# Router logits by token half in a two-layer decoder trunk, and the order of the steps up to the first gather

## The chip, the cores and the metric

The kernel runs on one core of a Trainium2 chip, alone. The metric is the device time of one execution in microseconds; the median of several runs counts. One further execution was recorded by the hardware profiler, and all rows below are from it. TensorE does the matrix products, VectorE and ScalarE the elementwise work, POOL (GpSimd) a little of it, and SyncE (SP) issues nearly all transfers.

## The reference, cut to what matters

The trunk has two layers with 256 tokens of width 1024, all in float32. A layer is a mixer of three branches, a cross-attention into 256 memory tokens, and a feed-forward part, each followed by a layer norm of `alpha * x + f(x)`. In the first layer the feed-forward part is dense; in the second one, which the change is about, it is a mixture of 8 experts with the best 2 taken for each token:

```python
def moe_swiglu(x, w_router, b_router, w_gu, w_down):
    logits = (x @ w_router).astype(jnp.float32) + b_router.astype(jnp.float32)
    top_vals, top_idx = lax.top_k(logits, TOP_K)
    top_w = jax.nn.softmax(top_vals, axis=-1)
    combine = jnp.sum(jax.nn.one_hot(top_idx, N_EXPERTS, dtype=jnp.float32) * top_w[..., None], axis=-2)
    out = jnp.zeros_like(x)
    for e in range(N_EXPERTS):
        out = out + combine[..., e:e + 1].astype(x.dtype) * swiglu(x, w_gu[e], w_down[e])
    return out
```

Here `x` is the output of the norm behind the cross-attention, `y * g + b` with `y` the normalized rows and `g`, `b` one value per channel.

## The kernel before, in words

**Precision by two parts.** A float32 operand of a big product is split into `hi`, its value rounded to the fast matmul type, and `lo`, the residual `raw - hi`; a product is three matmuls, hi x hi, hi x lo and lo x hi. The weights come as 1 MB tiles (`raw`, L242 to L256) by SyncE's queue. Each is used in halves of 128x1024: ScalarE makes `whi` (L218), VectorE makes `wlo` (L221). There are three buffers of each. In the last layer the raw tiles go through a long ring of 15 buffers, so that transfers run far ahead.

**The order.** A planner places the instructions of each engine by priority (mostly program order) and by its own estimate of durations, so an instruction of later code fills a gap where its inputs are there. Code under `tc.high_priority()` goes first; both norms and all that they call are written so. A `Line` (L230 to L239) pins a chain by hand: each call is issued behind the one before it on its engine. The norm has four such chains, `dv` for VectorE, `ac` for ScalarE, `te` for TensorE and `gp` for POOL. Instructions called through a Line are recorded at L238. `guard` (L225, L270) holds the next weight residuals back behind a given instruction of VectorE: the norm sets it to the next two, behind `shift(1)` (L343).

**The norm ahead of the experts** (`layer_norm_in`, L310, with kind "moe", called from `cross` at L1109). Tokens are in two halves, m = 0 and 1, with 128 tokens on the partitions. For each half VectorE adds up `y = alpha * x + f` (tile `lny`) and takes its statistics, POOL raises the variance to the power -0.5 (`brs`), and VectorE makes the shift (`bnb`, L327). ScalarE normalizes the rows in place (L347); TensorE transposes them by 128x128 blocks into four PSUM tiles, which hold two channel blocks of both halves each (L351). The affine part is then applied to the transposed blocks, one 128x256 operation per channel block, five on ScalarE and three on VectorE (`lnx`, L364 to L367), and TensorE takes the logits transposed, 8 experts on the partitions by 256 tokens: eight products with an 8-column stationary and 256 columns streamed (`pl`, L369). The affine part of the rows themselves (`x`, needed for the gather and the residual path) is done by POOL for half 0 (L354, L355) and by VectorE for half 1 (L356, L380). ScalarE rounds them to `xhi` (L382).

**The router** (`moe`, L1170). VectorE copies the logits from PSUM (`lgt`), TensorE transposes them back (L1189), VectorE adds the bias row (`lg`), compares all pairs (`eq`, `cmp`), sums to `rank` and takes `sel`, the two best. TensorE counts earlier tokens of each expert by triangular and all-ones matrices (L1213 to L1215); VectorE makes the token's `slot` in its expert, and `pe`, the 128x128 selection matrices (L1258, recorded at L238). The residuals of the rows, `xlo`, are made one in the shade of the counting (L1216) and one behind `pe` (L1260). `prepare` (L1253) gathers the rows of two experts by matmuls with `pe` (L1273), 16 with `xhi` and 16 with `xlo`; ScalarE and VectorE carry the results into `xg` (the casts). `weigh` (L1227) computes the two weights, and POOL scales `x` by alpha for the last norm (L1250).

**The experts.** For each of 8 experts and 7 blocks of 512 hidden columns, `gate_up` (L1292) runs two chains `pg` and `pu` over four weight halves each, then SiLU and product (`msl`); `down` (L1317) projects back, and `scatter` (L1329) adds the weighted rows to `x`.

**The earlier norm of the same layer.** Behind the mixer the norm of kind "xt" runs, with cross-attention keys as filling; then `cross` (L1043) does the last block of keys (L1052) and the query projection (L1054).

## Time and profile before

| | |
|---|---|
| median of 3 runs | 1942.06 us (1941.7 to 1943.23) |
| the profiled execution's own time | 1947.3 us |
| its span, first to last instruction | 1945.4 us |
| TensorE busy in the span | 1882.1 us (97%) |
| VectorE busy | 1532.6 us (79%) |
| ScalarE busy | 1283.2 us (66%) |
| POOL busy | 110.9 us (6%) |
| mean granted TensorE clock | 0.984 |

The engines' names in the rows are PE for TensorE's matmuls, PEld for its weight loads, DVE for VectorE, ACT for ScalarE, POOL for GpSimd and SP for SyncE. A matmul row gives rows * columns of the stationary operand and then partitions x columns of the result. A busy TensorE in these rows is not TensorE at its peak: matmuls overlap, and their ends are modelled. Times in the timelines are from the span's start; a merged row "x3" runs from the first start to the last end.

### The profile page before, as it was taken

Reading aid. Unit: us, or ns where it says so; the run is one execution under the profiler, and the core shown is the slowest. Engines: PE = TensorE matmul, PEld = TensorE weight load, DVE = VectorE, ACT = ScalarE, POOL = GpSimd, SP = SyncE. Lnnn points to the kernel's source line nnn. Section 1 sums busy time; section 2 is a strip of 40 time slices with the busy share of each in tenths; the row PEclk is TensorE's granted clock in tenths of the full one; section 3 lists DMA queues with packets and bytes.
Section 4 is the critical chain, followed back from the end, with each engine's and each line's share of the span. In section 5 each row is a group of like instructions: output and inputs, shape, how many; then the busy total and the mean of one; then the engine's idle time right before and its main releaser. Section 6 shows DMA issues by size and latency. Waiting matters only on the chain.

```text
span 1945.4 us, 27894 instructions
## 1 busy us (share of the span) xinstructions
PE 1882.1 (97%) x10672; PEld 1634.6 (84%) x10672; DVE 1532.6 (79%) x1976; ACT 1283.2 (66%) x1673; POOL 110.9 (6%) x111
## 2 busy tenths in 40 slices
PE   7999999999999999989899999999999999999996
PEld 7998998899989988877688888888888888888875
DVE  7774764794557755755899999999999999999987
ACT  5666554555444555544678787887777778788774
POOL 4030000100004300000200000000000000000000
PEclk9999999999999999989899999999999999999998
DMA  7324553544554343594499998999989999899970
GB/s 255 131 93 153 185 216 134 182 171 163 185 188 170 130 145 121 194 378 173 174 371 371 359 373 320 375 373 355 375 318 375 375 354 374 318 375 368 382 274 24
DMA packets 74924, 503.37 MB, mean 259 GB/s; under 512 B 9504, under 2 KB 11808, under 8 KB 15264
## 3 DMA queue, kind: packets, MB, share of 16 engines
q1 hardware_dynamic: 74496, 500.43, 68.6%
q8 instruction: 85, 1.39, 0.3%
q0 software_dynamic: 144, 1.05, 0.2%
q14 instruction: 55, 0.45, 0.1%
q10 hardware_dynamic: 144, 0.05, 0.0%
HBM read 498.34 MB, written 1.05 MB: 257 GB/s over the span
## 4 chain that ended last, share of the span: by engine, by line
PE 87%; DVE 8%; ACT 3%; issue 2%; DMA 0%; POOL 0%; ACTq 0%; DVEq 0%; POOLq 0%
PE ps L281 8%; PE ps L283 8%; PE ps L282 8%; PE pu L1302 5%; PE dn L450 5%; PE pu L1303 5%; PE pu L1301 5%; PE pg L1303 5%; PE pg L1302 5%; PE dn L451 5%; PE dn L452 5%; PE pg L1301 5%; DVE wlo L221 3%; PE acc L428 2%; PE acc L430 2%; PE acc L432 2%
## 5 line engine op out<-in xcount | busy, mean ns | idle before, releaser
L221 DVE TENSOR_TENSOR wlo<-raw,whi 128x1024 fp32r<-128x1024 f32 x926 | 1118.3, 1229 | 308.4 <-ACT whi L218 295.3
L218 ACT ACTIVATE whi<-raw 128x1024 fp32r<-128x1024 f32 x926 | 974.4, 1060 | 519.3 <-PE ps L282 187.5
L281 PE MATMUL ps<-xhi,whi 128*128 128x256 f32 x992 | 288.3, 291 | 14.8 <-ACT whi L218 14.8
L283 PE MATMUL ps<-xhi,wlo 128*128 128x256 f32 x992 | 286.4, 290 | 4.3 <-DVE wlo L221 4.3
L282 PE MATMUL ps<-xlo,whi 128*128 128x256 f32 x992 | 286.8, 289 | 0.0
L281 PEld LDWEIGHTS ps<-xhi,whi 128*128 128x128 f32 x992 | 194.8, 197 | 16.3 <-ACT whi L218 15.5
L283 PEld LDWEIGHTS ps<-xhi,wlo 128*128 128x128 f32 x992 | 194.8, 197 | 5.8 <-DVE wlo L221 5.1
L282 PEld LDWEIGHTS ps<-xlo,whi 128*128 128x128 f32 x992 | 195.3, 197 | 0.8 <-issue 0.3
L1302 PE MATMUL pu<-wlo,xg 128*128 128x512 f32 x448 | 176.1, 393 | 2.7 <-DVE wlo L221 2.7
L451 PE MATMUL dn<-wlo,hth 128*128 128x512 f32 x448 | 178.0, 400 | 0.1
L1302 PE MATMUL pg<-wlo,xg 128*128 128x512 f32 x448 | 176.6, 394 | 1.4 <-DVE wlo L221 1.4
L1303 PE MATMUL pg<-whi,xg 128*128 128x512 f32 x448 | 175.8, 392 | 0.6 <-DVE xg L1254 0.6
L1301 PE MATMUL pg<-whi,xg 128*128 128x512 f32 x448 | 175.2, 391 | 0.0
L1301 PE MATMUL pu<-whi,xg 128*128 128x512 f32 x448 | 175.1, 391 | 0.0
L1303 PE MATMUL pu<-whi,xg 128*128 128x512 f32 x448 | 174.8, 390 | 0.0
L452 PE MATMUL dn<-whi,htl 128*128 128x512 f32 x448 | 174.0, 391 | 0.0
L450 PE MATMUL dn<-whi,hth 128*128 128x512 f32 x448 | 139.5, 391 | 0.0
L1302 PEld LDWEIGHTS pu<-wlo,xg 128*128 128x128 f32 x448 | 84.1, 188 | 27.6 <-DVE wlo L221 6.6
L1302 PEld LDWEIGHTS pg<-wlo,xg 128*128 128x128 f32 x448 | 84.1, 188 | 24.1 <-DVE wlo L221 3.8
L1301 PEld LDWEIGHTS pu<-whi,xg 128*128 128x128 f32 x448 | 84.1, 188 | 17.9
L450 PEld LDWEIGHTS dn<-whi,hth 128*128 128x128 f32 x448 | 83.9, 188 | 17.8
L1301 PEld LDWEIGHTS pg<-whi,xg 128*128 128x128 f32 x448 | 84.2, 188 | 17.4
(520 smaller groups left out, 2869.5 us busy)
## 6 DMA issues: line engine op xcount, KB each, us to landing
raw<-in_w SPq DMA_DIRECT2D x462, 1024.0 KB, 4.9
lng<-in_ln SPq DMA_DIRECT2D x6, 512.0 KB, 6.4
lnb<-in_ln SPq DMA_DIRECT2D x6, 512.0 KB, 7.2
raw<-in_memt SPq DMA_DIRECT2D x2, 1024.0 KB, 4.7
raw<-in_xt SPq DMA_DIRECT2D x4, 256.0 KB, 5.7
raw<-in_w SPq DMA_DIRECT2D x2, 512.0 KB, 6.0
ux<-us SPq DMA_DIRECT2D x32, 32.0 KB, 2.1
yg<-ux SPq DMA_DIRECT2D x32, 32.0 KB, 1.9
```

The lines of the kernel that those rows point to most:

```text
L218: return A.activation(dst, src, AF.Copy, scale=scale)
L221: return V.tensor_sub(dst, src, hi.bitcast(F32))
L281: T.matmul(ps, whi, xhi, start=first, stop=False)
L282: T.matmul(ps, whi, xlo, start=False, stop=False)
L283: return T.matmul(ps, wlo, xhi, start=False, stop=last)
L428: T.matmul(accs[m][n], ah, wh, start=first, stop=False)
L450: T.matmul(ps, ah, wh, start=first, stop=False)
L451: T.matmul(ps, ah, wl, start=False, stop=False)
L452: return T.matmul(ps, al, wh, start=False, stop=last)
L1301: T.matmul(ps, xg[0][:, k, :], wh, start=(k == 0), stop=False)
L1302: T.matmul(ps, xg[0][:, k, :], wl, start=False, stop=False)
L1303: T.matmul(ps, xg[1][:, k, :], wh, start=False, stop=(k == KD - 1))
```

## The change

It does four things.

- The logits are taken by token half in natural layout: the transposed blocks of the normalized rows, without the affine part, are copied out of PSUM as `xft` (one 128x512 copy on ScalarE and one on VectorE for each half), and each is the 128-column stationary of a product with 8 streamed columns, 16 in all. Tokens lie on the partitions of the result, so that `lgt` and the transposes back are gone.
- The affine part is folded into the router on the chip: behind the last keys of the last layer, eight matmuls make the row `b @ w_router`, which is added to the bias `br`, and one VectorE operation multiplies the router by `g`.
- A new order: the chains of `route` put the rows' affine part, now all on VectorE, between the steps of the logits; `xlo` of both halves is made behind `pe`; `guard` becomes a list, and prepare() holds the first weight residual behind `xlo` and the next two behind the casts of the high part.
- POOL's scaling of `x` by alpha becomes two ScalarE operations in the first expert, and the transfer of the routing constants is issued ahead of the norm.

```diff
@@ -222,7 +222,7 @@
 
     pos = [0]
     ahead = [None, 0]
-    guard = [None, 0]
+    guard = []
...
                 hi_of(hi, r)
-                if guard[1] > 0:
-                    guard[1] -= 1
-                    Line(guard[0])(lo_of, lo, r, hi)
+                if guard:
+                    Line(guard.pop(0))(lo_of, lo, r, hi)
                 else:
                     lo_of(lo, r, hi)
...
         xhi = xp.tile(sh, F32R, tag="xhi", name="xhi")
-        xlo = xp.tile(sh, F32R, tag="xlo", name="xlo")
+        if kind == "xt":
+            xlo = xp.tile(sh, F32R, tag="xlo", name="xlo")
+        else:
+            xft = xp.tile([P, 2, KD, P], F32, tag="xlo", name="xft")
...
         shift(1)
-        guard[:] = [dv.prev, 2]
-        for m in range(2):
+        guard[:] = [dv.prev] * 2
+        def transposed(m):
             for n in range(2):
                 y = ys[m]
                 ac(A.activation, y[:, H[n]], y[:, H[n]], AF.Identity, scale=rss[m], bias=nbs[m])
                 for k in range(4 * n, 4 * n + 4):
                     if m == 0 and k % 2 == 0:
                         pts.append(psa.tile([P, 2, 2, P], F32, tag="acc", name="pt"))
-                    te(T.transpose, pts[k // 2][:, k % 2, m, :], y[:, k * P:(k + 1) * P], ident)
+                    if kind == "moe":
+                        dst = pts[2 * m + n][:, k % 4 // 2, k % 2, :]
+                    else:
+                        dst = pts[k // 2][:, k % 2, m, :]
+                    te(T.transpose, dst, y[:, k * P:(k + 1) * P], ident)
+
         if kind == "moe":
-            pl = psa.tile([P, 512], F32, tag="acc", name="pl")
-            gp(GP.tensor_mul, x[:, 0, :], ys[0], g)
-            gp(GP.tensor_add, x[:, 0, :], x[:, 0, :], b)
-            dv(V.tensor_mul, x[:, 1, :], ys[1], g)
+            return route(xhi, ys, g, b, xft, r, transposed, pts, te, ac, dv, lp)
+        for m in range(2):
+            transposed(m)
         for q in range(4):
...
-                if kind == "moe" and k >= 5:
-                    dv(V.tensor_scalar, xk, pk, gt[:, k:k + 1], bt[:, k:k + 1], op0=ALU.mult, op1=ALU.add)
+                ac(A.activation, xf[:, kk, :], pts[q][:, kk].rearrange("p m t -> p (m t)"), AF.Identity,
+                   scale=gt[:, k:k + 1], bias=bt[:, k:k + 1])
...
+    def route(xhi, ys, g, b, xft, r, transposed, pts, te, ac, dv, lp):
+        pl = [psw.tile([P, 512], F32, tag="wk", name="pl") for _ in range(2)]
+        lg, sel, rank = (chosen[:, i] for i in range(3))
+        cmp_, eq = (lp.tile([P, 2, E, E], F32, name=n, bufs=1) for n in ("cmp", "eq"))
+
+        def logits(m, between):
+            transposed(m)
+            for n in range(2):
+                k4 = slice(4 * n, 4 * n + 4)
+                pt = pts[2 * m + n].rearrange("p a b t -> p (a b) t")
+                if n == 0:
+                    ac(A.copy, xft[:, m, k4], pt)
                 else:
...
-            dv(V.tensor_add, x[:, 1, :], x[:, 1, :], b)
-            for m in (1, 0):
-                ac(hi_of, xhi[:, m], x[:, m])
-        if kind == "moe":
-            return xhi, xlo, pl, dv
-        return xhi, xlo
+                    between()
+                    dv(V.tensor_copy, xft[:, m, k4], pt)
+                for k in range(4 * n, 4 * n + 4):
+                    te(T.matmul, pl[m][:, :E], xft[:, m, k], r[:, k, :], start=(k == 0), stop=(k == KD - 1))
+
+        def scaled(m):
+            dv(V.tensor_mul, x[:, m, :], ys[m], g)
+
+        def moved(m):
+            dv(V.tensor_add, x[:, m, :], x[:, m, :], b)
+            ac(hi_of, xhi[:, m], x[:, m])
+
+        logits(0, lambda: None)
+        logits(1, lambda: scaled(0))
+        moved(0)
+        scaled(1)
+        for m in range(2):
+            dv(V.tensor_add, lg[:, m], pl[m][:, :E], br)
+        sh4 = [P, 2, E, E]
+        lo4 = lg.unsqueeze(2).to_broadcast(sh4)
+        le4 = lg.unsqueeze(3).to_broadcast(sh4)
+        dv(V.tensor_tensor, eq, lo4, le4, op=ALU.is_equal)
+        dv(V.tensor_tensor, cmp_, lo4, le4, op=ALU.is_gt)
+        dv(V.tensor_mul, eq, eq, R("lt").rearrange("p (e f) -> p e f", e=E).unsqueeze(1).to_broadcast(sh4))
+        dv(V.tensor_add, cmp_, cmp_, eq)
+        dv(V.tensor_reduce, rank, cmp_, axis=AX.X, op=ALU.add)
+        dv(V.tensor_scalar, sel, rank, 1.5, None, op0=ALU.is_lt)
+        moved(1)
+        xlo = xp.tile([P, 2, D], F32R, tag="xlo", name="xlo")
+        return xhi, xlo, dv
 
     lnt = cp.tile([P, L, 6, KD], F32, name="lnt")
+    chosen = cp.tile([P, 3, 2, E], F32, name="chosen")
+    rout = []
+
+
+    def R(name):
+        if not rout:
+            rout.append(cp.tile([P, NCT - NCA], F32, tag="ca", name="cr"))
+            nc.sync.dma_start(rout[0], cst_in[:, NCA:])
+        return rout[0][:, CC[name][0] - NCA:CC[name][1] - NCA]
+
     wr = cp.tile([P, KD, E], F32, name="wr")
     br = cp.tile([P, E], F32, name="br")
     ones = cp.tile([P, P], F32, name="ones")
@@ -1050,6 +1097,13 @@
                     A.copy(vv[:, m, n * 512:(n + 1) * 512], va[m])
 
             keys(mt, 7 if l else 1, 8, kt_, w)
+            if l == L - 1:
+                pb = psw.tile([P, 512], F32, tag="wk", name="pb")
+                for k in range(KD):
+                    T.matmul(pb[:, :E], lnt[:, l, 3, k:k + 1].to_broadcast([P, P]), wr[:, k, :], start=(k == 0),
+                             stop=(k == KD - 1))
+                V.tensor_add(br, br, pb[:, :E])
+                V.tensor_mul(wr, wr, lnt[:, l, 2, :].unsqueeze(2).to_broadcast([P, KD, E]))
             qt = wk.tile([P, KD, S], F32, tag="xq", name="xqt", bufs=1)
             ws_gemm(8, KD, xt, lambda ob, ps: A.copy(qt[:, ob, :], ps))
 
@@ -1106,6 +1160,7 @@
             accs = acc4()
             xs_gemm(accs, (o_hi, o_lo), KD, D)
         if l == L - 1:
+            R("lt")
             return layer_norm(l, 1, lambda m, n: accs[m][n], None, "moe", wr)
         kt_, w, end = keys(mt, 0, 1)
         xt = layer_norm(l, 1, lambda m, n: accs[m][n], end)
@@ -1167,7 +1222,7 @@
         keys(mt, 5, 6, kt_, w)
         return xt, sp, par
 
-    def moe(l, xn_hi, xn_lo, pl, dv):
+    def moe(l, xn_hi, xn_lo, dv):
         with ExitStack() as es:
             mp = es.enter_context(tc.tile_pool(name="moe", bufs=1, reuse_waits="tile"))
             wk = es.enter_context(tc.tile_pool(name="moew", bufs=2, reuse_waits="tile"))
@@ -1175,45 +1230,19 @@
             psd = es.enter_context(tc.tile_pool(name="mpd", bufs=2, space=PSUM))
             pst = es.enter_context(tc.tile_pool(name="mpt", bufs=2, space=PSUM))
 
-            cr = cp.tile([P, NCT - NCA], F32, tag="ca", name="cr")
-            nc.sync.dma_start(cr, cst_in[:, NCA:])
-
-            def R(name):
-                return cr[:, CC[name][0] - NCA:CC[name][1] - NCA]
-
-
-            lgt = mp.tile([E, S], F32, name="lgt")
-            dv(V.tensor_copy, lgt, pl[:E, :S])
-            ps = pst.tile([P, 512], F32, tag="tr", name="ps")
-            for m in range(2):
-                T.transpose(ps[:, m * E:(m + 1) * E], lgt[:, m * P:(m + 1) * P], ident[:E, :E])
-            lg = mp.tile([P, 2, E], F32, name="lg")
-            dv(V.tensor_add, lg, ps[:, :2 * E].rearrange("p (m e) -> p m e", m=2),
-               br.unsqueeze(1).to_broadcast([P, 2, E]))
-
+            lg, sel, rank = (chosen[:, i] for i in range(3))
             sh = [P, 2, E]
-            sh4 = [P, 2, E, E]
 
             def t(name, s=sh):
                 return mp.tile(s, F32, name=name)
 
-            cmp_, eq, rank, sel, fst, sec = t("cmp", sh4), t("eq", sh4), t("rank"), t("sel"), t("fst"), t("sec")
-            lo4 = lg.unsqueeze(2).to_broadcast(sh4)
-            le4 = lg.unsqueeze(3).to_broadcast(sh4)
-            ltm = R("lt").rearrange("p (e f) -> p e f", e=E)
-            dv(V.tensor_tensor, eq, lo4, le4, op=ALU.is_equal)
-            dv(V.tensor_tensor, cmp_, lo4, le4, op=ALU.is_gt)
-            dv(V.tensor_mul, eq, eq, ltm.unsqueeze(1).to_broadcast(sh4))
-            dv(V.tensor_add, cmp_, cmp_, eq)
-            dv(V.tensor_reduce, rank, cmp_, axis=AX.X, op=ALU.add)
-            dv(V.tensor_scalar, sel, rank, 1.5, None, op0=ALU.is_lt)
+            fst, sec = t("fst"), t("sec")
 
 
             ps = pst.tile([P, 512], F32, tag="tr", name="ps")
             T.matmul(ps[:, 0:E], R("triu"), sel[:, 0, :], start=True, stop=True)
             T.matmul(ps[:, E:2 * E], ones, sel[:, 0, :], start=True, stop=False)
             T.matmul(ps[:, E:2 * E], R("triu"), sel[:, 1, :], start=False, stop=True)
-            dv(lo_of, xn_lo[:, 1], x[:, 1], xn_hi[:, 1])
             slot = t("slot")
             dv(V.scalar_tensor_tensor, slot, ps[:, 0:2 * E].rearrange("p (m e) -> p m e", m=2), 1.0, sel,
                op0=ALU.add, op1=ALU.mult)
@@ -1247,7 +1276,6 @@
                 cnt = mp.tile([P, 1], F32, name="cnt")
                 V.tensor_reduce(cnt, ps[:, 0:E], axis=AX.X, op=ALU.max)
                 V.tensor_copy(cnti, cnt)
-                GP.tensor_scalar(x, x, ALPHA, None, op0=ALU.mult)
 
 
             def prepare(ne, slot_col, dv=None):
@@ -1257,7 +1285,9 @@
                     for m in range(2):
                         dv(V.tensor_scalar, pe[:, m, e, :], iota, 1.0, slot_col(m, e), op0=ALU.add, op1=ALU.is_equal)
                 if isinstance(dv, Line):
-                    dv(lo_of, xn_lo[:, 0], x[:, 0], xn_hi[:, 0])
+                    for m in range(2):
+                        dv(lo_of, xn_lo[:, m], x[:, m], xn_hi[:, m])
+                    guard[:] = [dv.prev]
                 xg = [[wk.tile([P, KD, P], F32R, tag=f"xg{i}", name=f"xg{i}", bufs=2) for i in range(2)]
                       for e in range(ne)]
                 w = ne * P
@@ -1279,6 +1309,8 @@
                                 A.copy(dst, ps[:, :, e, :])
                             else:
                                 dv(V.tensor_copy, dst, ps[:, :, e, :])
+                    if isinstance(dv, Line) and i == 0:
+                        guard.extend([dv.prev] * 2)
                 res = []
                 for e in range(ne):
                     ps = pst.tile([P, 512], F32, tag="tr", name="ps")
@@ -1358,6 +1390,8 @@
                     prev, ht = ht, gate_up(xg, gsrc(e, nb))
                     if prev is not None:
                         down(pd, prev, nb - 1, dsrc(e, nb - 1))
+                    if e == 0 and nb in (2, 3):
+                        A.activation(x[:, nb - 2], x[:, nb - 2], AF.Copy, scale=ALPHA)
                 if e + 1 < E and not ready:
                     ready = prepare(2, lambda m, j: slot[:, m, e + 1 + j:e + 2 + j])
                 down(pd, ht, NEB - 1, dsrc(e, NEB - 1))
```

## Rows read from the trace of the kernel before

**Rows 1.** Busy time by stretch, inside the experts (engine columns: busy us, instructions):
```profile
core 0: us, PE busy (x) PEld busy (x) DVE busy (x) ACT busy (x) POOL busy (x), PEclk, DMA share, GB/s
957.00:1057.00 100.00, 99.78 (x450) 82.06 (x451) 92.68 (x87) 79.61 (x83) 0.00 (x0) 1.00 0.96 367
1420.00:1540.00 120.00, 119.81 (x555) 98.48 (x554) 111.05 (x113) 94.33 (x106) 0.00 (x0) 1.00 0.92 351
```

**Rows 2.** Waits from 945 us on: waiter <- awaited: us in total, times, longest.
```profile
ACT whi L218 <- PE pu L1303: 70.0, 128, 1.1
```

**Rows 3.** Timeline of TensorE (start us, us, what, count, [idle before <- releaser]):
```profile
919.93 0.39 PE L452 MATMUL acc<-whi,m_lo 128*128 128x512 f32 x1
922.44 1.82 PE L238 MATMUL pt<-cst,lny 128*128 128x128 f32 x8 [2.12 <-ACT lny L238]
926.70 1.97 PE L238 MATMUL pt<-cst,lny 128*128 128x128 f32 x8 [2.44 <-ACT lny L238]
...
937.84 0.60 PE L1213 MATMUL ps<-sel,cr 128*128 128x8 f32 x2 [1.85 <-DVE sel L238]
...
938.71 0.58 PE L1215 MATMUL ps<-sel,cr 128*128 128x8 f32 x2
940.43 3.43 PE L1273 MATMUL ps<-pe,xhi 128*128 128x256 f32 x16 [1.14 <-DVE pe L238]
```

**Rows 4.** Timeline of VectorE from the norm to the eighth half:
```profile
916.28 0.69 DVE L238 SCALAR_TENSOR_TENSOR lny<-x,acc 128x512 f32<-128x512 f32 x1 [1.76 <-PE acc L452]
...
923.50 2.29 DVE L238 SCALAR_TENSOR_TENSOR bnb<-bmv,brs 128x1 f32<-128x1 f32 x1 [0.75 <-POOL brs L238]
925.72 5.64 DVE L221 TENSOR_TENSOR wlo<-raw,whi 128x1024 fp32r<-128x1024 f32 x3
931.29 1.21 DVE L238 TENSOR_TENSOR x<-lny,lng 128x1024 f32<-128x1024 f32 x1
...
936.23 0.29 DVE L238 TENSOR_TENSOR eq<-lg 128x128 f32<-128x128 f32 x1
...
937.61 0.17 DVE L238 TENSOR_SCALAR sel<-rank 128x16 f32<-128x16 f32 x1
937.69 1.22 DVE L221 TENSOR_TENSOR xlo<-x,xhi 128x1024 fp32r<-128x1024 f32 x1
939.33 0.17 DVE L238 SCALAR_TENSOR_TENSOR slot<-ps,sel 128x16 f32<-128x16 f32 x1 [0.41 <-PE ps L1215]
...
955.93 1.23 DVE L221 TENSOR_TENSOR wlo<-raw,whi 128x1024 fp32r<-128x1024 f32 x1 [1.47 <-ACT whi L218]
```

**Rows 5.** Timeline of POOL:
```profile
923.44 2.34 POOL L238 TENSOR_TENSOR x<-lny,lng 128x1024 f32<-128x1024 f32 x1
925.86 3.29 POOL L238 TENSOR_TENSOR x<-x,lnb 128x1024 f32<-128x1024 f32 x1
...
941.71 5.40 POOL L1250 TENSOR_SCALAR x<-x 128x2048 f32<-128x2048 f32 x1 [8.99 <-DVE xlo L221]
```

**Rows 6.** Timeline of VectorE, first norm of the same layer:
```profile
834.87 3.49 DVE L221 TENSOR_TENSOR wlo<-raw,whi 128x1024 fp32r<-128x1024 f32 x3
```

**Rows 7.** Busy time by stretch, after and before the first gather matmul:
```profile
940.43:957.16 16.73, 16.07 (x83) 13.90 (x83) 12.71 (x33) 11.86 (x20) 5.40 (x1) 0.91 0.36 127
923.50:940.43 16.93, 9.32 (x36) 4.46 (x35) 15.65 (x24) 6.20 (x9) 5.67 (x3) 0.70 0.17 62
```

**Rows 8.** Timeline of ScalarE:
```profile
935.36 2.00 ACT L218 ACTIVATE xhi<-x 128x1024 fp32r<-128x1024 f32 x2 [3.88 <-DVE x L238]
...
953.07 1.28 ACT L1305 ACT_TABLE_LOAD   x1
```

**Rows 9.** Timeline of TensorE, first norm of the same layer:
```profile
833.68 0.58 PE L281 MATMUL ps<-xhi,whi 128*128 128x256 f32 x1 [6.29 <-ACT whi L218]
```

**Rows 10.** Busy time by stretch, for the granted clock (PEclk, third from the right):
```profile
835.00:840.00 5.00, 4.28 (x20) 3.99 (x20) 3.36 (x3) 1.06 (x1) 0.00 (x0) 0.50 1.02 429
...
923.00:924.00 1.00, 1.00 (x5) 0.72 (x4) 0.50 (x1) 0.09 (x1) 1.00 (x2) 0.50 0.00 0
...
944.00:945.00 1.00, 1.00 (x9) 0.96 (x9) 1.00 (x3) 0.27 (x1) 1.00 (x1) 1.00 0.00 0
```

More of the change, by code (lines that the diff above doesn't have):

```diff
@@ L354, in layer_norm_in @@
-            gp(GP.tensor_mul, x[:, 0, :], ys[0], g)
-            gp(GP.tensor_add, x[:, 0, :], x[:, 0, :], b)
-            dv(V.tensor_mul, x[:, 1, :], ys[1], g)
+            return route(xhi, ys, g, b, xft, r, transposed, pts, te, ac, dv, lp)
+        for m in range(2):
+            transposed(m)
         for q in range(4):
-            if kind == "xt":
-                xf = lp.tile([P, 2, S], F32, tag="lnx", name="lnx")
+            xf = lp.tile([P, 2, S], F32, tag="lnx", name="lnx")
             for kk in range(2):
-                xk = xf[:, kk, :] if kind == "xt" else lp.tile([P, S], F32, tag="lnx", name="lnx")
@@ L362, in layer_norm_in @@
                 k = 2 * q + kk
-                pk = pts[q][:, kk].rearrange("p m t -> p (m t)")
-                if kind == "moe" and k >= 5:
-                    dv(V.tensor_scalar, xk, pk, gt[:, k:k + 1], bt[:, k:k + 1], op0=ALU.mult, op1=ALU.add)
-                else:
-                    ac(A.activation, xk, pk, AF.Identity, scale=gt[:, k:k + 1], bias=bt[:, k:k + 1])
-                if kind == "moe":
-                    T.matmul(pl[:E, :S], r[:, k, :], xk, start=(k == 0), stop=(k == KD - 1))
@@ L370, in layer_norm_in @@
-            if kind == "xt":
-                hs = xhi[:, 2 * q:2 * q + 2, :]
-                dv(V.tensor_copy, hs, xf)
-                dv(lo_of, xlo[:, 2 * q:2 * q + 2, :], xf, hs)
-        if kind == "xt":
-            with tc.high_priority(offset=-LATER), tc.issue_after(dv.prev.ins):
-                for m in range(2):
-                    V.tensor_mul(x[:, m, :], ys[m], g)
-                    V.tensor_add(x[:, m, :], x[:, m, :], b)
-        else:
-            dv(V.tensor_add, x[:, 1, :], x[:, 1, :], b)
-            for m in (1, 0):
-                ac(hi_of, xhi[:, m], x[:, m])
@@ L383, in layer_norm_in @@
-        if kind == "moe":
-            return xhi, xlo, pl, dv
-        return xhi, xlo
-    lnt = cp.tile([P, L, 6, KD], F32, name="lnt")
+                ac(A.activation, xf[:, kk, :], pts[q][:, kk].rearrange("p m t -> p (m t)"), AF.Identity,
+                   scale=gt[:, k:k + 1], bias=bt[:, k:k + 1])
+            hs = xhi[:, 2 * q:2 * q + 2, :]
+            dv(V.tensor_copy, hs, xf)
+            dv(lo_of, xlo[:, 2 * q:2 * q + 2, :], xf, hs)
+        with tc.high_priority(offset=-LATER), tc.issue_after(dv.prev.ins):
+            for m in range(2):
+                V.tensor_mul(x[:, m, :], ys[m], g)
+                V.tensor_add(x[:, m, :], x[:, m, :], b)
@@ new lines, in layer_norm_in @@
+        return xhi, xlo
+    def route(xhi, ys, g, b, xft, r, transposed, pts, te, ac, dv, lp):
[9 more added lines that the diff above has]
+                    ac(A.copy, xft[:, m, k4], pt)
+                else:
+                    between()
[25 more added lines that the diff above has]
+        return xhi, xlo, dv
@@ L1259, in prepare @@
                 if isinstance(dv, Line):
-                    dv(lo_of, xn_lo[:, 0], x[:, 0], xn_hi[:, 0])
+                    for m in range(2):
+                        dv(lo_of, xn_lo[:, m], x[:, m], xn_hi[:, m])
+                    guard[:] = [dv.prev]
                 xg = [[wk.tile([P, KD, P], F32R, tag=f"xg{i}", name=f"xg{i}", bufs=2) for i in range(2)]
```

1 line of the change is left out of this document (removed).

## The prediction, made before the changed kernel ran

> **What bounds the kernel now.** I read the table of 40 slices first, for the stages, then the stretches by engine, the waits behind the change, the timeline of each engine around it, and last the norm of the same layer where the folding will go. Two regimes meet here. In the experts TensorE is busy for 99.78 of 100 us and 119.81 of 120 us at the full clock, with VectorE close behind at 92.68 of 100 and the transfers at 0.92 to 0.96 [rows 1]; the commonest wait there is ScalarE's split waiting for TensorE to release a buffer [rows 2]. So the experts run at TensorE's pace, and a start that comes 1 us earlier ends 1 us earlier. Ahead of them lies a serial stretch: TensorE's last projection matmul ends at 920.3 us, and between it and the first gather matmul at 940.43 there are only transposes, logits and counts with gaps [rows 3]. This is what the change rewrites.
>
> The hand-over also matters. The last place where TensorE visibly waits for a residual (the wlo half that VectorE makes) is the eighth half of the first expert: it starts at 955.93 and ends at 957.16 [rows 4]. I measure everything to that point, because beyond it both kernels run alike.
>
> **The change, part by part.** The times stand on the profiled execution, 1947.3 us with a span of 1945.4; the median shown is 1942.06, 5.2 us less, and the difference of the sum is taken off the median.
>
> Part 1, the work taken from POOL. POOL scaled and shifted token half 0 from 923.44 to 929.15 [rows 5]. Beside it the one-element shift took 2.29 us, and three residuals took 5.64 us [rows 4] where three took 3.49 us in the earlier norm [rows 6]. That is 2.1 and 2.15 us of VectorE standing still behind POOL. The change leaves POOL only its two small powers there, so the shift ends about 923.7 instead of 925.8.
>
> Part 2, the path to the gather. The guard is now a list; the two entries set in the norm are overwritten in prepare() before any weight half is split, so the first three residuals no longer stand between the shift and the router: the first comes after the two xlo, the next two after the casts of the high part. The path from 923.7, each step by its row: the transposes of half 0 end at 924.26 [rows 3]; one 128x512 copy out of PSUM on VectorE, 0.69 by the nearest operation of that shape [rows 4], to 924.95; four 8-column matmuls with a 128-column stationary, 0.22 each by the spacing of the count matmuls, (938.71 - 937.84) / 4 [rows 3], to 925.85; eight transposes of half 1, which the order puts behind them, 1.85 by their row [rows 3], to 927.7; the second copy, 928.4; x0's addition and x1's product, 1.21 each [rows 4], which the chain puts ahead of the logits and under which the last four matmuls hide, to 930.8; two additions of the bias row, 0.35, to 931.2. From there the tail is as before: 936.23 to 937.61 for the comparisons up to the selection, 1.38; 1.72 from its start to the slot, with x1's addition (1.21) in the shade of the count matmuls; 1.10 from slot to gather [rows 3, 4]. That gives 935.4, and 0.2 for handshakes 935.6: a head start of 4.8 us. Ends: with two of the residuals squeezed in after all it is 4.8 - 2.3 = 2.5; with TensorE at its full clock on twelve of these instructions, 0.1 less each, 6.0.
>
> [...] The weight load of a count matmul begins a 0.22 us slot [rows 3]. [...]
>
> Part 3, what is put off. The work that no longer stands ahead of the gather stands behind it. From the gather's start to the end of the eighth half VectorE was busy for 12.71 of 16.73 us [rows 7]. To this come one more xlo (1.2) and three residuals (3.49) [rows 4, 6]: 17.4 us, already 0.7 more than the stretch was long. The floor of what is given back is thus 0.7. The ceiling takes all of the old idle time along, 16.73 - 12.71 = 4.0, and gives 4.7. Most of this idle time was waiting that the later arrival absorbs: 1.47 us before the eighth half [rows 4], while ScalarE loaded a table for 1.28 [rows 8], and gaps around the gather's casts that the extra xlo fills. I keep 0.7 of it: 1.4 given back. TensorE is what is late next: its first products with wlo stand in its queue and wait for VectorE, and ScalarE's whi wait for TensorE to free the ring of three.
>
> Part 4, the folding. Eight 8-column matmuls and two small VectorE operations between the last keys and the query projection. By the 0.22 spacing they take 1.8 us. They are hidden if they fall into the gap before the query projection, where TensorE idles 6.29 us for its first weight half [rows 9]; without this cover they cost 1.8 and a few tenths on VectorE, 2.1 at most. They cannot gain. I take 0.2, because they need nothing that arrives late. [...]
>
> Part 5, moved pieces. The scaling of x by alpha leaves POOL (5.40 us in the gather's shade [rows 5]) for two ScalarE passes of about 1.0 [rows 8] in the first expert, where ScalarE is busy for 79.61 of 100 us [rows 1]. ScalarE's next whi waits behind each, then VectorE, then TensorE; the ring of three halves covers it. 0 to 1.0, taken as 0.2. On SyncE the constants' transfer is issued earlier in the program, ahead of the norm's two rows; the transfers were busy for 0.17 and 0.36 of the two halves of this stretch [rows 7], which is the cover. Uncovered it is one more row of a few hundred bytes per partition ahead of the norm's own two, which TensorE's last projection hides.
>
> Sum: -4.8 + 1.4 + 0.2 + 0.2 = -3.0 us, so 1942.06 - 3.0 = 1939.1 us, or 0.15%.
>
> **The rivals.** First, the head start is kept whole. Then TensorE sets the pace behind the gather: the 1.2 us that it lost at the eighth half may vanish as well. For it speaks that VectorE idled 4.0 of 16.73 us there [rows 7], and that small operations of the weighting can slip behind the residuals; against it the 17.4 us of work. It gives -4.8 + 0.4 = -4.4 up to -5.6: 1936.5 to 1937.7.
>
> Second, all is given back: the old waits stay and the extra work adds to them, 4.7 against 4.8. It gives -0.1 + 0.4, about 1942.4 us. For it: the whi of the eighth half was late because of ScalarE, not of VectorE [rows 4, 8]. Against it: VectorE then arrives later than that whi.
>
> [...]
>
> That the change doesn't do what it says is part of the second: were the gather held by something else, nothing would move.
>
> **How the numbers follow.** A measurement of this kernel can tell about 0.2%, 3.9 us, from no change. Forecast (gain of 1.5 to 4.3): 0.52, of which 0.05 lies beyond 3.9. Head start kept: 0.28. All given back: 0.13. Slower: 0.07. Faster is 0.28 + 0.05 = 0.33, same 0.47 + 0.13 = 0.60, slower 0.07. The likeliest time is 1939.1; its own range is 1937.7 to 1940.6. The range for 8 in 10 reaches into the first rival down to 1936.4 and takes in the second up to 1942.6; it leaves out the third and some of the first.
>
> **What would show it.** In the changed profile: no POOL multiplication at 923; a shift of 0.16 us; the first gather matmul about 15.3 us behind the last projection matmul (20.1 before); the three residuals behind the xlo; the eighth residual about 18 us behind the gather's start; the eight folding matmuls inside the gap of the earlier norm. The prediction is wrong if the eighth residual comes within 16.8 us of the gather (first rival), if it takes 21 us (second), if the clock is at 0.5 for 10 us behind the gather (third), or if the stretch before the query projection grows by over 1 us (the folding was on the path).

## The result, and the profile after

| | before | after |
|---|---|---|
| median | 1942.16 us (4 runs) | 1964.27 us (1961.0 to 1965.84, 4 runs) |
| ratio, 95% interval | | 1.0112 [1.0097, 1.0127] |
| profiled execution, its span | 1947.3 us, 1945.4 us | 1961.0 us, 1959.2 us |
| mean granted clock | 0.984 | 0.987 |

The changed kernel is some 22 us slower; 1939.1 was predicted, 1942.6 was the upper end. The runs of one kernel spread by up to 9 us, with the granted clock (of the kernel before, in its runs beside E1 to E12, all below 1944 us had 0.985 or more and all above 1948 had 0.983 or 0.984), and one run of E11, which took 3764.79 us, is in no ratio.

Read first by stages. The next two fences give the busy time of four stretches, first of the kernel before, then of the changed one: from the end of the mixer's gated products to the end of the last projection, to the first gather product, to the first scatter (the end of expert 0, whose scatter comes in expert 1's first block), and to the end. Columns as in [rows 1].

```profile
818.77:920.32 101.55, 93.47 (x528) 82.70 (x527) 54.59 (x76) 47.20 (x77) 1.67 (x3) 0.95 0.68 269
920.32:940.43 20.11, 10.38 (x40) 5.24 (x41) 17.98 (x30) 8.97 (x13) 6.24 (x4) 0.73 0.14 52
940.43:1067.12 126.69, 125.97 (x579) 104.32 (x580) 114.56 (x127) 99.63 (x112) 5.40 (x1) 0.99 0.89 335
1067.12:1945.44 878.32, 859.03 (x3890) 700.75 (x3888) 803.75 (x780) 674.60 (x728) 1.99 (x2) 0.99 0.88 337
```
```profile
813.82:916.63 102.81, 95.65 (x545) 84.06 (x543) 54.84 (x78) 47.31 (x77) 1.58 (x3) 0.95 0.68 266
916.63:932.30 15.67, 10.56 (x54) 9.76 (x55) 11.00 (x26) 7.47 (x10) 0.65 (x2) 0.64 0.01 2
932.30:1064.72 132.42, 130.76 (x579) 105.81 (x580) 118.84 (x131) 103.35 (x116) 0.00 (x0) 0.98 0.88 331
1064.72:1959.22 894.50, 876.29 (x3890) 703.47 (x3888) 807.92 (x780) 674.03 (x728) 1.97 (x2) 0.99 0.88 331
```

The second rows are what the change was made for: 15.67 us against 20.11. The last rows hold the loss. The same 3890 matmuls, at the same granted clock of 0.99, with TensorE busy nearly all the time in both, take 894.50 us instead of 878.32. TensorE's idle time in it has not grown (18.2 us, 19.3 before); every matmul comes a little later behind the one before it. The changed kernel's answer to [rows 1], and a stretch of the kernel before beside it (the second fence), say it once more: fewer matmuls in the same time at a full clock (441 for 449), and fewer GB/s (356 for 365), because the weights are used more slowly. TensorE's busy share hides it, 99.72 against 99.51.

```profile
1300.00:1400.00 100.00, 99.72 (x441) 80.27 (x440) 92.33 (x87) 77.05 (x82) 0.00 (x0) 1.00 0.94 356
1420.00:1540.00 120.00, 119.81 (x545) 96.97 (x544) 109.48 (x111) 93.17 (x105) 0.00 (x0) 1.00 0.92 346
```
```profile
1300.00:1400.00 100.00, 99.51 (x449) 81.48 (x449) 93.21 (x88) 78.79 (x84) 0.00 (x0) 1.00 0.96 365
```

From start to start, the 128x512 products of the experts come every 227 ns before and every 233 ns after (medians over some 2700 gate and up products). The same two figures stand side by side in the trace of the kernel before, for the same shape: 227 ns in the experts, 233 ns in the feed-forward part of the first layer. What differs with them, in all groups of 512 columns but the scatter's few products, is a number that no row shows: the distance between the addresses of a product's two operands in a partition (stationary less streamed), modulo 256 bytes. In the experts the weights are streamed and the gathered rows are stationary. As the compiled programs place them:

```
                       weights whi  gathered rows xg  distance mod 256  512 columns
before                 45792        199136             0                227 ns
after                  45984        197088            64                233 ns
before, feed-forward                                 224                233 ns
```

The change makes the new tile `chosen`, 192 bytes a partition, in the constants' pool, and all pools that are stacked behind it move by 192 bytes. From the experts' pool it takes six small tiles (2240 bytes), so the gathered rows move by 192 - 2240 = -2048. The weights have moved by 192, the rows by a multiple of 256.

### The profile page after: what moved, and what is told of

Its sections match the earlier page's. It is cut to its first block, busy times and chain, and to the rows that moved or that the text cites. A ratio compares the mean times of both kernels' runs of the same rounds, so it can differ in the third digit from the quotient of the medians.

```text
span 1959.2 us, 27949 instructions
## 1 busy us (share of the span) xinstructions
PE 1900.6 (97%) x10702; PEld 1637.1 (84%) x10702; DVE 1535.5 (78%) x1979; ACT 1284.5 (66%) x1674; POOL 102.9 (5%) x108
## 4 chain that ended last, share of the span: by engine, by line
PE 86%; DVE 7%; ACT 3%; issue 2%; DMA 1%; POOL 1%; SPq 0%; DVEq 0%; ACTq 0%; POOLq 0%
PE ps L280 8%; PE ps L282 8%; PE ps L281 8%; PE pg L1335 5%; PE pu L1334 5%; PE pg L1334 5%; PE pu L1335 5%; PE pg L1333 5%; PE pu L1333 5%; PE dn L497 5%; PE dn L499 5%; PE dn L498 5%; DVE wlo L221 3%; PE acc L475 2%; PE acc L477 2%; PE acc L479 2%
## 5 line engine op out<-in xcount | busy, mean ns | idle before, releaser
L1335 PE MATMUL pg<-whi,xg 128*128 128x512 f32 x448 | 177.9, 397 | 0.6 <-DVE xg L1282 0.6
L1333 PE MATMUL pu<-whi,xg 128*128 128x512 f32 x448 | 177.3, 396 | 0.0
L1333 PE MATMUL pg<-whi,xg 128*128 128x512 f32 x448 | 177.3, 396 | 0.0
L1335 PE MATMUL pu<-whi,xg 128*128 128x512 f32 x448 | 177.0, 395 | 0.0
```

The costliest lines, as they stand in the source:

```text
L1333: T.matmul(ps, xg[0][:, k, :], wh, start=(k == 0), stop=False)
L1335: T.matmul(ps, xg[1][:, k, :], wh, start=False, stop=(k == KD - 1))
```

## The experiments

E1 to E7 and E12 only widen tiles that exist, so that addresses move and nothing else: every engine has the instructions of the base, one by one. The base is the kernel before in E1, E3, E5, E6 and E12, and the changed kernel in E2, E4 and E7.

**E1, the kernel before with the fault put in.**

```diff
-            cnti = mp.tile([P, 1], I32, name="cnti")
+            cnti = mp.tile([P, 17], I32, name="cnti")[:, :1]
```

> The kernel before with one small tile of the experts' pool widened by 64 bytes (cnti, 4 to 68 bytes a partition), so that the gathered rows and the hidden rows stand 64 bytes further behind the weight ring; no instruction is added, removed or moved. Theory A (the change lost its time by an address: 512-column matmuls whose two operands stand a multiple of 256 bytes apart come every 227 ns, others every 233): the experts' matmuls move from 227 to 233 ns, about 985 us x 5.3/228 = 22 to 23 us more, about 1964 to 1966 us. Theory B (the new order of the steps, the router or the clock lost it): no change, 1942 us.

Measured 1963.94 us, ratio 1.0099 [1.0083, 1.0114]: 19 us of the 22, from 64 bytes. Its two expert stretches:

```profile
937.02:1067.59 130.57, 129.95 (x579) 105.79 (x580) 115.25 (x127) 99.60 (x112) 5.39 (x1) 0.98 0.87 327
1067.59:1962.16 894.57, 876.53 (x3890) 702.84 (x3888) 807.61 (x780) 674.05 (x728) 1.99 (x2) 0.99 0.88 331
```

The last row is the changed kernel's to 0.1 us in 894, without any of the change.

**E2, the changed kernel with the fault taken out** (`[P, 49]` for cnti, 192 bytes).

> The changed kernel with the same small tile widened by 192 bytes, so that the gathered rows stand a multiple of 256 bytes from the weight ring again, as they did before the change; nothing else. Theory A: the expert matmuls are back at 227 ns, 22 to 23 us less than the changed kernel, 1940 to 1942 us: what is left of the change's own gain at the gather (about 3 us) less what the 192 bytes cost in the dense layers (480 matmuls of 512 columns x 6 ns, less 570 of 256 columns x 2 ns, 1.7 us). Theory B: 1964 us, as the changed kernel.

Measured 1944.47 us against 1945.51 before on the same chip, ratio 1.0002 [0.9993, 1.0011]. The experts are back at 227 ns, and the last stretch is as short as before; of the loss nothing is left, but of a gain there is nothing either.

```profile
1065.26:1942.80 877.54, 858.12 (x3890) 700.89 (x3888) 803.50 (x780) 674.37 (x728) 1.97 (x2) 0.99 0.89 337
```

**E3, the whole layout moved with the change's 192 bytes.**

```diff
-    br = cp.tile([P, E], F32, name="br")
+    br = cp.tile([P, E + 48], F32, name="br")[:, :E]
```

> The kernel before with br, a tile of the constants' pool, widened by 192 bytes: weight ring, normalized rows and the experts' pools all move by the same 192 bytes, as in the change, and the experts' operands keep their distance. Theory A: only the dense layers' pools at the other end of memory change their distance: 480 matmuls of 512 columns x 6 ns more, 570 of 256 columns x 2 ns less, 1.7 us more: about 1943 to 1944 us. Theory C (where the weight ring itself stands decides, whatever the distance): about 1962 to 1966 us.

Measured 1945.33 us, ratio 1.0007 [0.9996, 1.0018]. Where the weights stand by themselves does not bring the loss. In the trace the dense groups whose distance went from 0 to 64 (memory and gate products) went from 227 to 233 ns at 512 columns and from 120 to 118 at 256; the size in time, 1.4 us, fits the 1.7 but is within the interval.

**E4, the changed kernel with every distance as before** (E2, and `chosen` as `[P, 4, 2, E]`, 256 bytes).

> The changed kernel with chosen rounded up from 192 to 256 bytes and the small tile of the experts' pool widened by 192: every pair of operands stands as far apart, modulo 256 bytes, as in the kernel before. Theory A: 1.7 us less than the run with the experts' 192 bytes alone, 1938.5 to 1940.5 us: this is what the change's own edits are worth, 2 to 4 us faster than before. Theory B: 1964 us.

Measured 1944.62 us, ratio 0.9997 [0.9985, 1.0009], -0.6 us with 2.3 on either side. This is what the change's own edits are worth, and it is less than the 3 us that both the prediction and this expectation gave. Its stretches show why:

```profile
818.19:920.07 101.88, 94.72 (x545) 84.18 (x543) 54.86 (x78) 47.30 (x77) 1.67 (x3) 0.95 0.68 268
920.07:937.06 16.99, 11.91 (x55) 11.25 (x55) 11.08 (x27) 7.47 (x10) 0.65 (x2) 0.57 0.01 1
937.06:1066.94 129.88, 128.07 (x580) 105.24 (x581) 118.08 (x131) 103.25 (x116) 0.00 (x0) 0.98 0.89 337
1066.94:1945.22 878.28, 859.02 (x3890) 700.35 (x3888) 803.55 (x780) 674.48 (x728) 1.97 (x2) 0.99 0.89 337
```

The experts are as before to 0.04 us. 3.1 us are won up to the gather (16.99 for 20.11), and 3.2 are lost between gather and first scatter (129.88 for 126.69; E3 has 127.64).

**E5, which multiple counts** (the kernel before, `[P, 33]` for cnti, 128 bytes).

> The kernel before with the same small tile of the experts' pool widened by 128 bytes, so that gathered and hidden rows stand 128 bytes off the multiple of 256 from the weight ring; nothing else. No trace so far has a pair of operands at 128. Theory A1 (the distance counts modulo 256 bytes): experts at 233 ns, ratio to before about 1.010, as with 64 bytes. Theory A2 (it counts modulo 128 bytes): experts at 227 ns, ratio 1.000.

Measured 1962.05 us, ratio 1.0093 [1.0070, 1.0115]; 232 ns, and 441 matmuls in 100 us, as in the changed kernel. So of the two it is theory A1, with 256 bytes, that fits, and 128 bytes off cost what 64 did (1.0093 and 1.0099).

```profile
1300.00:1400.00 100.00, 99.73 (x441) 80.50 (x440) 92.28 (x86) 77.62 (x83) 0.00 (x0) 1.00 0.94 359
```

**E6, the rule used for a gain.**

```diff
-    x = xp.tile([P, 2, D], F32, name="x")
+    x = xp.tile([P, 2 * D + 8], F32, name="x")[:, :2 * D].rearrange("p (m d) -> p m d", m=2)
...
-            cnti = mp.tile([P, 1], I32, name="cnti")
+            cnti = mp.tile([P, 57], I32, name="cnti")[:, :1]
```

> The kernel before with x widened by 32 bytes (a tile that nothing streams through TensorE), which moves the normalized rows xhi and xlo and the feed-forward's hidden rows by 32 bytes against the weight ring, and the experts' small tile widened by 224, so that the experts keep their distance. Theory A, read the other way for 256 columns: 3072 matmuls of 256 columns go from 119.9 to 118 ns (5.8 us less), 264 of the feed-forward's 512 columns from 233 to 227 (1.5 us less), 96 of 512 columns on the normalized rows from 227 to 233 (0.6 us more): 6.7 us less if TensorE sets the pace in all of these, ratio 0.9965; 2 to 3 us less, if the weights' split or its transfers set it in half of them. Rival (the 256-column difference is only in how records are spaced, and time is set elsewhere): ratio 1.000.

Measured 1938.52 us against 1946.93 before, ratio 0.9968 [0.9955, 0.9982]: 6.2 us less for the 6.7 expected, by 32 bytes. The 256-column products of the normalized rows come every 117 ns (120 before), the feed-forward's every 227 to 228 (233 before). The expected sum left out 576 products of 256 columns in the mixer that moved from 32 to 0 and came up to 3 ns later, some 1 us in all.

**E7, the same in the changed kernel** (E4, the 32 bytes in x, `[P, 41]` for cnti).

> The changed kernel with every distance as in the kernel before (chosen 256 bytes, experts' pad) and the same 32 bytes in x. Theory A: as much below the aligned changed kernel (ratio 0.9997 to before) as the run of the kernel before with 32 bytes in x is below before: ratio 0.996 to 0.998; the two runs with 32 bytes differ by what the change's own edits are worth, 0 to 1 us by the aligned run, 3 us by the prediction.

Measured 1937.04 us, ratio 0.9958 [0.9942, 0.9974]. It is faster than both kernels. Against E6 the change's edits are worth 0.1%, with intervals that overlap.

**E8, E9 and E10, where the head start goes.** Behind the gather ScalarE has new work: two scalings by ALPHA inside the gather, and Exp behind the first SiLU, which means two more table loads (E4 has three of 1.28 us there, the kernel before has one). E8 took both back. E9 and E10 edited the scaling alone, and the planner then moved Exp ahead of the first SiLU as well.

```diff
-                    if e == 0 and nb in (2, 3):
-                        A.activation(x[:, nb - 2], x[:, nb - 2], AF.Copy, scale=ALPHA)
...
                 V.tensor_copy(cnti, cnt)
+                GP.tensor_scalar(x, x, ALPHA, None, op0=ALU.mult)
```

> The aligned changed kernel (chosen 256 bytes, experts' 192) with two of its moves taken back: the ALPHA scaling of x is one instruction on POOL again, not two on ScalarE, and the seven small steps up to the Exp of the two best logits are issued during the gather, so that Exp comes ahead of the first SiLU. Theory D (the head start is kept to the gather, and given back behind it by ScalarE, which carries two scalings of 1.06 us in the gather and two more table loads of 1.28 us): from the first gather product to the first scatter 129.8 us becomes 128.0 to 128.8, the idle time of 0.12 and 0.44 us before the second block's products goes, ratio to before 0.9985 to 0.9993. [...]

> The aligned changed kernel (chosen 256 bytes, experts' 192) with the ALPHA scaling of x as one instruction on POOL again, behind the routing weights, as before the change; nothing else is edited, but the planner then also puts Exp ahead of the first SiLU by itself. Theory D (ScalarE's two scalings in the gather and its two more table loads give back part of the head start): the idle 0.12 and 0.44 us before the second block's products goes, and so does most of the 0.76 us at a residual; from the first gather product to the first scatter 129.8 us becomes 128.0 to 129.0, ratio to before 0.998 to 0.9993. [...]

> The same edit on the aligned changed kernel with 32 bytes in x: its instructions are those of the run with ALPHA on POOL, one by one, and only addresses differ. Theories A and D together: 0.9958 less 0.0004 to 0.0015, so 0.9943 to 0.9954, the fastest of all. If only A holds: 0.9958.

Measured: E8 1947.71 us, ratio 1.0013 [1.0001, 1.0024]; E9 1946.31 us, 1.0011 [0.9999, 1.0023]; E10 1936.73 us, 0.9965 [0.9953, 0.9978]. From gather to first scatter they take 134.49, 132.25 and 132.38 us, against 129.88 and 129.58 in E4 and E7. Theory D missed: the idle time at the second block was gone, but a bigger wait had come. E9 on VectorE, POOL and TensorE:

```profile
942.10 4.48 DVE L221 TENSOR_TENSOR wlo<-raw,whi 128x1024 fp32r<-128x1024 f32 x2
946.50 1.40 DVE L238 CAST xg<-ps 128x256 fp32r<-128x256 f32 x4
...
939.81 6.28 POOL L1279 TENSOR_SCALAR x<-x 128x2048 f32<-128x2048 f32 x1 [6.99 <-DVE xlo L221]
...
946.97 0.79 PE L1336 MATMUL pg<-whi,xg 128*128 128x512 f32 x1 [2.38 <-DVE xg L238]
```

POOL scales x from 939.81 to 946.09, and two residuals beside it take 4.48 us instead of 2.35 (E8 has two at that, most of it behind POOL's end); the gather's casts wait behind them, and TensorE waits 2.38 us for the casts. In E8 the victim was an operation on 16 columns:

```profile
936.55 3.29 DVE L1260 TENSOR_TENSOR sec<-chosen,fst 128x16 f32<-128x16 f32 x1
...
940.91 2.35 DVE L221 TENSOR_TENSOR wlo<-raw,whi 128x1024 fp32r<-128x1024 f32 x2
```

It takes 0.17 us in the changed kernel. The casts beside POOL's scaling were not held: in E8 one took 0.42 us and two took 0.74, as in E11, where POOL does no scaling. In E8 TensorE's granted clock, 1.00 from 938.7 to 942.1, fell in the gap and was 0.50 for 6.8 us from 942.1 on. In E9 the gap (944.60 to 947.00) has 0.97, and the products behind it took 0.79 and 0.63 us, where they take 0.39 at the full clock. So the ALPHA scaling is better on ScalarE, where the change put it, and these runs don't price ScalarE's part.

**E11, Exp alone put early** (E7, with weigh()'s steps from `fst` to Exp moved into a function `differ`, which E8 has too).

```diff
                     guard[:] = [dv.prev]
+                    with tc.issue_after(dv.prev.ins):
+                        differ()
```

> The aligned changed kernel with 32 bytes in x, ALPHA left on ScalarE as the change has it, and only the seven small steps up to Exp issued during the gather, ahead of the first SiLU. The two runs with ALPHA on POOL showed VectorE standing behind POOL's scaling for some 2 to 3 us, so they did not price ScalarE's part. Theory D: without the two extra table loads the idle 0.16 and 0.44 us before the second block's products goes and the 0.76 us at a residual with it or in part: from the first gather product to the first scatter 129.6 us becomes 128.3 to 129.1, ratio 0.9950 to 0.9955 against 0.9958. Rival (the seven steps, 0.17 us each, stand between VectorE's gather copies and cost as much there): 129.4 us or more, ratio 0.9958 or above.

In the trace theory D holds: 127.54 us for the stretch. The first fence is E7, idle time of TensorE by groups from 950 to 1062 us (last column: idle before, and what ended it); the second has the stretch from gather to scatter, of E6, E7 and E11 in turn:

```profile
L1334 PE MATMUL pg<-wlo,xg 128*128 128x512 f32 x50 | 19.7, 394 | 0.8 <-DVE wlo L221 0.8
L1334 PE MATMUL pu<-wlo,xg 128*128 128x512 f32 x50 | 19.6, 392 | 0.5 <-DVE wlo L221 0.5
L1333 PE MATMUL pu<-whi,xg 128*128 128x512 f32 x50 | 19.6, 392 | 0.2 <-ACT whi L218 0.2
...
L497 PE MATMUL dn<-whi,hth 128*128 128x512 f32 x56 | 17.6, 392 | 0.4 <-ACT whi L218 0.4
```
```profile
932.04:1058.91 126.87, 126.14 (x580) 104.47 (x580) 114.44 (x127) 99.64 (x112) 5.40 (x1) 0.99 0.88 336
933.10:1062.68 129.58, 127.36 (x580) 104.22 (x581) 118.02 (x131) 103.47 (x116) 0.00 (x0) 0.99 0.89 337
928.63:1056.17 127.54, 127.40 (x579) 105.33 (x580) 118.09 (x131) 100.77 (x114) 0.00 (x0) 0.98 0.90 343
```

TensorE is idle for 0.14 us in it (127.54 - 127.40), for 2.2 in E7 (129.58 - 127.36). In time it does not show: 1938.42 us, ratio 0.9969 [0.9959, 0.998], which is the rival's value (0.9958 or above) and outside theory D's 0.9950 to 0.9955. Its fastest run, 1931.67 us, is the fastest of the study, and the granted clock stood at 0.982 in half of its runs. So the times do not show the 2 us that the trace shows.

**E12, from what the distance is taken.**

```diff
-                xg = [[wk.tile([P, KD, P], F32R, tag=f"xg{i}", name=f"xg{i}", bufs=2) for i in range(2)]
+                xg = [[wk.tile([P, KD * P + 16], F32R, tag=f"xg{i}", name=f"xg{i}", bufs=2)[:, :KD * P].rearrange("p (k q) -> p k q", k=KD) for i in range(2)]
```

> The kernel before with each buffer of the gathered rows widened by 64 bytes: for the experts of even number the high parts (xg0) stay at a multiple of 256 bytes from the weights and the low parts (xg1) are 128 off; for the odd ones the high parts are 64 off and the low parts 192; the hidden rows, another 256 bytes on, keep their distance. It tells what the distance is taken from. Theory A3 (a matmul's own two operands): for even experts the two products on xg0 come every 227 ns and the third, on xg1, every 232 to 233. Theory A4 (the operand that is streaming against the weights being loaded for the next matmul): the second, during which xg1 is loaded, comes at 233 and the third at 227. For odd experts all three are slow in either. By both, two in three of the gate and up products are slow, some 9 us more than before, ratio 1.004 to 1.005.

Measured 1953.92 us, ratio 1.0054 [1.0037, 1.0072], so the size fits. The order does not: for even experts the three products came every 230, 232 and 233 ns (means), for odd ones every 232, 230 and 234. Neither theory gives this. In the even experts the slow ones are the second, which A4 named, and the third, which A3 named, and the scatter's few products, which stand at distance 0 among the experts', slow down with them in the changed kernel (medians of 228 and 233 ns, 227 before), E1 and E5; so a neighbour's operand seems to count beside a product's own. The odd experts' second product, at 230, does not fit that either, and the question stays open.

## Why the prediction was wrong, point by point

**The step that failed** is in the first paragraph: "the experts run at TensorE's pace, and a start that comes 1 us earlier ends 1 us earlier", with its sequel, "beyond it both kernels run alike". TensorE does set the pace, but the pace was taken as given. The sum has a term for every instruction of the diff and none for the new tile's 192 bytes, which moved the weights against the gathered rows. E1 puts this at 19.3 us (0.0099 x 1945.51); E3 puts the dense layers' share at 1.4, which is within its interval. The last stretch, well inside the part in which "both kernels run alike", took 16.2 us more (894.50 for 878.32). Neither of the first two rivals had it; slower, the side on which it came out, stood at 0.07. A second term was too small: of the head start, part 3 gave 1.4 us back, and the runs gave back 2.7 (129.58 in E7 for 126.87 in E6). So the change's own edits are worth 0.6 us with 2.3 on either side (E4) and not 3.0.

Part 1 was right. POOL has only its two powers of 0.55 us; the shift takes 0.16 us and ends 3.3 us behind the projection (3.4 predicted):

```profile
919.73 0.16 DVE L238 SCALAR_TENSOR_TENSOR bnb<-bmv,brs 128x1 f32<-128x1 f32 x1 [0.75 <-POOL brs L238]
```

Part 2 was right in the changed kernel, 15.67 us to the gather for 15.3 predicted, and a little large with the distances mended: 16.99 and 16.66 in E4 and E7, so 3.1 to 3.5 won instead of 4.8, inside its 2.5 to 6.0. How near the changed kernel came is luck in part. The difference goes with the clock, which the prediction priced for this path only in its end of 6.0: behind the projection TensorE still had 1.00 for 4.5 us in the changed kernel, for 3.0 in E7 and for 2.3 in E4, and the longer it lasted, the shorter the path. The first row is of the changed kernel, the second of E4:

```profile
916.63:921.10 4.47, 2.32 (x18) 1.88 (x18) 3.38 (x8) 4.43 (x7) 0.55 (x1) 1.00 0.00 0
920.07:922.30 2.23, 0.11 (x2) 0.11 (x2) 2.16 (x5) 2.23 (x4) 0.00 (x0) 1.00 0.00 0
```

One reading was off by a little: the eight transposes of half 1 stand at 1.97 us in their row, not 1.85. One price was low: it counted records as products. A float32 product of 8 columns is two matmul records here, so the eight of half 1 took 3.58 us; x1's scaling covered most of it. The second row is the folding's:

```profile
924.34 3.58 PE L238 MATMUL pl<-wr,xft 128*128 128x8 f32 x16
...
816.72 1.62 PE L1103 MATMUL pb<-wr,lnt 128*128 128x8 f32 x14
```

Per record that is 0.22 us at a granted clock of 0.50 (3.58 / 16) and 0.116 at 1.00 (1.62 / 14). The prediction took the row's 0.22 us for a whole product, where the row has two records for each product and a clock of 0.50.

Part 3 was right at its own mark and wrong in its range. The eighth residual ends 17.90 us behind the gather (about 18 predicted, 16.73 before):

```profile
948.97 1.23 DVE L221 TENSOR_TENSOR wlo<-raw,whi 128x1024 fp32r<-128x1024 f32 x1 [1.16 <-ACT whi L218]
```

But the stop there, "the last place where TensorE visibly waits", held for the kernel before alone. In the changed one Exp slipped behind the first SiLU, so that ScalarE loads three tables where one load stood, and its whi are late into the second block:

```profile
946.10 1.28 ACT L1337 ACT_TABLE_LOAD   x1
...
948.96 1.28 ACT L1266 ACT_TABLE_LOAD   x1
...
960.17 1.28 ACT L1337 ACT_TABLE_LOAD   x1
```

E7 against E11 prices that at 2.0 us in the traces (129.58 - 127.54). The clock does not explain it, as E11 had the low clock for longer: 0.50 for 5.7 us behind the gather's start, where E7 had it for 3.4.

```profile
933.10:936.40 3.30, 3.30 (x15) 3.30 (x16) 3.30 (x4) 2.08 (x3) 0.00 (x0) 0.50 0.00 0
936.50:937.50 1.00, 1.00 (x10) 1.00 (x10) 1.00 (x4) 0.91 (x4) 0.00 (x0) 1.00 0.00 0
```
```profile
928.63:934.30 5.67, 5.67 (x25) 5.59 (x26) 5.67 (x14) 3.08 (x6) 0.00 (x0) 0.50 0.00 0
```

With it most of the head start is given back, as in the second rival, though by ScalarE and not by the old waits; without it 0.7 us are (127.54 against 126.87 in E6), the floor of part 3.

Part 4 was right in size and wrong in place: the folding ran ahead of the first transposes of the earlier norm, not in the gap before the queries. The stretch from gated products to projection takes 101.48 us in E7 and 101.40 in E6, 101.88 in E4 and 101.98 in E3: nothing that can be read, for 0.2 predicted. The changed kernel itself has 102.81 for 101.55 before, over the 1 us that was named as a sign. E3, with its distances there and without the folding, has 101.98, and 0.8 us is what that stretch can vary by with the same instructions and addresses (E1 has 100.74); so the sign does not show the folding on the path.

Part 5: both scalings were placed in the gather and not in the blocks where the code stands:

```profile
933.52 1.06 ACT L1394 ACTIVATE x<-x 128x1024 f32<-128x1024 f32 x1 [1.59 <-DVE xlo L221]
...
934.74 1.06 ACT L1394 ACTIVATE x<-x 128x1024 f32<-128x1024 f32 x1
```

E11 has them there too and loses nothing by it. That POOL's scaling was "in the gather's shade" held before the change only; with the new order E9 and E10 pay 2.4 and 2.8 us for it.

First rival: no, the eighth residual came at 17.9 us, not within 16.8. Third, the clock at 0.5 for 10 us behind the gather: no, and a low clock did not make the loss. The granted clock stood at 0.50 from 921.1 on for 17.1 us, and so through the whole stretch below; 5.9 of them lie behind the gather's start, 2.9 in the kernel before. In the dense products behind, from 938.2 on, it was 1.00 again. If half of the time at 0.50 is lost (a record of 0.22 us there took 0.116 at 1.00), the 3 us more of it are an estimate of 1.5 us at most, of a loss of 22. In E4, with 5.7 us of it behind the gather's start, the same working gives up to 1.4 of the 3.2 us that were lost there.

```profile
921.00:938.00 17.00, 14.04 (x66) 13.59 (x66) 13.43 (x26) 6.23 (x10) 0.10 (x1) 0.50 0.01 1
```

## What to carry to other kernels

A diff that adds, drops or resizes a tile can move the pools behind it (here by 192 bytes): compare the addresses of the big products' operands, not the instructions alone, before believing a profile in which each matmul is 2 to 3% slower (233 ns for 227) and nothing waits. Two groups of one shape with different spacing in one trace (227 and 233 ns here) are the sign, and padding of some bytes is the test and the remedy (192 in E2, 32 in E6). A gain at the head of a stage is to be followed to the end of the first unit of work behind it, because a small operation that changes its place (Exp behind SiLU) can take it back there (2.0 us in the traces of E7 and E11).

## What the runs showed of the hardware that was not expected

- In these traces the spacing of fast-float32 products at the full clock goes with the distance of their operands' addresses modulo 256 bytes. At 512 columns: 227 ns from start to start at 0, some 233 at 32, 64, 128 and 224 (medians of the groups from 231 to 236). For the dense layers' products of 256 columns it is the other way: 120 ns at 0, 117 to 118 at 32, 192 and 224. The groups of the traces of before, after and E1 to E7 agree, but for three: the scatter's 64 products, which stand at 0 among the experts' and slow down with them, the gather's products of 256 columns (118 to 122 at every distance), and one group of the mixer at 32 (up to 120). The mechanism was not found.
- POOL's scaling of 2048 columns (6.28 to 6.37 us in E8 to E10) held VectorE up for 2 to 3 us: at two residuals in E9 and E10 (4.48 and 4.49 us for 2.35), and in E8 at an operation of 16 columns (3.29 us for 0.17).
